# Block sums on VectorE, an earlier second product's transfer, and plain weight loads in a four-stage fp32 network step

## The chip, the core and the metric

The kernel runs on one core of a Trainium2 chip. TensorE multiplies, VectorE and ScalarE work element by element, POOL (GpSimd) does so too and issues the transfers of its queue, SP only issues transfers. The metric is the time of one execution on the device in microseconds.

## The reference, cut to what matters

640 tokens (512 latent, 128 context) of width 1024 pass through two layers. Each layer is a SwiGLU feed-forward, a token mixer (attention in layer 0, a long convolution in layer 1), and a second feed-forward, each with a modulation ahead of it and a layer norm behind. All is float32.

```python
def swiglu(h, w1, w2):
    g, u = jnp.split(h @ w1, 2, axis=-1)
    return (jax.nn.silu(g) * u) @ w2          # 1024 -> 2 x 2816 -> 1024

h = modulate(x, mod[:, 0], mod[:, 1])
f = swiglu(h, P['ffn_w1'][i, 0], P['ffn_w2'][i, 0])
x = layer_norm(DEEPNORM_ALPHA * x + 0.5 * mod[:, 2][:, None] * f, ...)
```

There are four feed-forwards: (layer 0, 0), (0, 1), (1, 0) and (1, 1). The modulation vectors `mod` come from one product of the condition with a 1024 x 9216 matrix per layer.

## The kernel before, in words

**Precision.** A float32 product is made of three passes over operands cut in a high and a low half (`hi`, `lo`): hi x hi, hi x lo, lo x hi. For a weight unit the high half `wh` comes by a transfer on POOL's queue that rounds it (`w_dma`, L115); the low half `wl` is made by `w_split`: ScalarE writes minus the high half into a new buffer (L127), and a second transfer of the same weights, accumulating, adds the full value (L128). Activations and block sums are cut by `split`: ScalarE copies the high half (L95), VectorE subtracts it (L96).

**Buffers and order.** All weight tiles, and the tiles `sw` below, share 8 buffers of 8 KB per partition (tag `w`). Every engine runs its instructions strictly in the order in which the program emits them; the order is written out by hand, and `w_get` splits units ahead as long as fewer than three are alive. `wlim` bounds how far weights may be loaded.

**Feed-forwards of layer 0** (`ffn`). The hidden layer has 22 columns of 128 in four parts of 6, 6, 6 and 4. For each column one unit of w1 (1 MB) is multiplied in two halves of 320 tokens (`ffn1`, L563, 96 matmuls); after a part's columns come four units of w2 (768 KB, `w2a`, L524, 72 matmuls each). Beside the work runs a background job, `bg_step`: a 512 KB piece of the modulation matrix (`ar`, double-buffered, issued by POOL at L243) is reduced on VectorE in two passes (L257). A column carries two steps; a w2 unit of the first two parts of feed-forward (0, 1) carries four. That feed-forward is the "prior" one: the block stages follow it.

**Feed-forwards of layer 1** (`ffn_s`), called block stages here. Columns 0 to 2 and 21 are computed as above. The 18 others go by a Strassen form in seven half-size products (`s_unit`): 84 matmuls at L669 of 128x128 weights with 320 tokens, each product of 12. Its weights are the four blocks a11, a12 (gate), a21, a22 (up) of a column, three of them as such (a11, a12, a22) and four sums s1 = a21 + a22, s2 = s1 - a11, s3 = a11 - a21, s4 = a12 - s2. `s_weights(c, nxt)` prepares them in four steps p0 to p3 during the column before; `hooks[i]` runs a step after product i. The raw blocks come by `s_load` on SP's queue into tiles `sr`. A block as such goes the way of a weight unit (copy, minus copy, accumulating transfer, L619 to L621); a sum is made on POOL or VectorE (L628, L635, L636, L645) and cut by `split`. The first product's result is copied by ScalarE (L685); further adds are VectorE's (L678, L699, L709).

Three columns make a part. Then `second` multiplies by two units `w2c` (768 KB; two of 1 MB, `w2b`, at the end): 16 groups of 9 matmuls at L524, eight for each unit; step `between[n]` runs after group n. The first of the two `w2c` units is loaded at `hooks[4]` of the part's second column and the other at `hooks[0]` of the third; the first is split at `hooks[2]` of the third, the other when `second` begins. In the last part, the next unit is column 21's w1 (1 MB).

Of the kernel before, what the change touches and what calls it, by code (L numbers as in the profile page):

```python
# [9 lines left out]
F32 = mybir.dt.float32  # L10
# [14 lines left out]

PARTS7 = [(0, 3), (3, 6), (6, 9), (9, 12), (12, 15), (15, 18), (18, 22)]
# [18 lines left out]
class Kernel:  # L45
# [63 lines left out]
    def w_dma(self, upto):  # L109
        nc = self.nc  # L110
        while self.wd < min(upto, self.wlim):
            i = self.wd
            src, shape = self.units[i]
            r = self.wp.tile(shape, F32R, tag="w", name="wh")
            nc.gpsimd.dma_start(out=r, in_=src)  # L115
            self.raw[i] = r
            self.wd += 1

    def w_split(self):
# [4 lines left out]
        shape = self.units[i][1]  # L124
        hi = self.raw.pop(i)
        lo = self.wp.tile(shape, F32R, tag="w", name="wl")
        self.nc.scalar.activation(out=lo, in_=hi.bitcast(F32), func=AF.Copy, scale=-1.0)  # L127
        self.nc.gpsimd.dma_start(out=lo, in_=self.units[i][0], accum_op=ALU.add)  # L128
# [5 lines left out]
    def w_first(self):  # L134

        i = self.wd
        src, shape = self.units[i]
# [459 lines left out]
    def s_load(self, blocks):  # L597

        for c, g, r in blocks:
            x = self.sp.tile([P, 4, P], F32, tag="sr", name="sr", bufs=5)  # L600
            self.nc.sync.dma_start(out=x, in_=self.I["w1s"][self.sf, c, g, r])
            self.sraw[c, g, r] = x

    def s_weights(self, c, nxt):

        nc = self.nc
        A = self.sraw
        st = {}
        self.sops[c] = ops = {}

        def slot(names):
            t = self.wp.tile([P, 4, 4, P], F32R, tag="w", name="sw")
            for i, n in enumerate(names):
                ops[n] = (t[:, i], t[:, 2 + i])

        def block(n, g, r):
            h, l = ops[n]
            x = A.pop((c, g, r)) if n == "a22" else A[c, g, r]
            nc.scalar.activation(out=h, in_=x, func=AF.Copy)  # L619
            nc.scalar.activation(out=l, in_=x, func=AF.Copy, scale=-1.0)  # L620
            nc.gpsimd.dma_start(out=l, in_=self.I["w1s"][self.sf, c, g, r], accum_op=ALU.add)  # L621

        def p0():
            st["s"] = self.sp.tile([P, 2, 4, P], F32, tag="s13", name="s13")
            st["d"] = self.sp.tile([P, 4, P], F32, tag="s24", name="s24")
            slot(("a11", "a12"))
            block("a11", 0, 0)
            nc.gpsimd.tensor_tensor(out=st["s"][:, 1], in0=A[c, 1, 0], in1=A[c, 1, 1], op=ALU.add)  # L628
            block("a12", 0, 1)
            if nxt is not None:  # L630
                self.s_load([(nxt, 0, 0)])
# [1408 lines left out]
```

## Time and profile before

| | us |
|---|---|
| median of 3 runs (2885.68 to 2892.03) | 2889.41 |
| profiled execution | 2896.11 |
| its span | 2893.1 |
| TensorE busy | 2648.9 (92%) |
| VectorE busy | 1709.7 (59%) |
| ScalarE busy | 1043.8 (36%) |
| POOL busy | 887.7 (31%) |

The span is that from the first to the last instruction of the profiled execution; 3.0 us lie around it. TensorE's granted clock is 0.960 of full speed over the span. POOL's queue moves 359.11 MB, SP's and the other hardware queue 89.72 MB. A busy share is an average over stages; what an idle stretch costs is read where it lies.

### The profile page before, as it was taken

The page shows a single profiled execution, that of the slowest core. Times are in us where ns is not written, and L with a number is a line of the kernel's source. Part 1 is how long each engine was busy: PE and PEld are TensorE (multiplying, and loading weights), DVE is VectorE, ACT ScalarE, POOL GpSimd, SP SyncE. Part 2 cuts the span into 40 slices and gives each one's busy share as a digit, 9 for nine tenths or more (in the row PEclk, how much of TensorE's full clock was granted, in tenths as well). Part 3 has the DMA queues.
Part 4 walks back from the last instruction along what each step waited for, and adds up shares of the span by engine and source line. Part 5 has one row for each costly group of instructions (what it writes and reads, how often), then busy time and mean ns, then how long its engine had stood idle before and what let it go on. Part 6 is the DMA issues. An engine that isn't in the chain of part 4 may idle for free.

```text
span 2893.1 us, 43816 instructions
## 1 busy us (share of the span) xinstructions
PE 2648.9 (92%) x16970; PEld 2505.6 (87%) x16970; DVE 1709.7 (59%) x3564; ACT 1043.8 (36%) x1916; POOL 887.7 (31%) x1126
## 2 busy tenths in 40 slices
PE   8799999999899988979998999989999898888887
PEld 3689999999548988979998999989999898888887
DVE  6846554449763556655377556546349758655554
ACT  4752212236773312111244333335323344333332
POOL 3521221143114211212153222224129643222223
PEclk9899999999999999989998999999999999999998
DMA  7877987862105678688645655564753544665552
GB/s 241 215 204 215 254 244 217 230 158 61 46 1 153 166 214 237 194 242 233 181 98 117 136 123 137 121 150 117 181 157 111 171 114 86 135 141 127 127 123 69
DMA packets 118214, 451.66 MB, mean 156 GB/s; under 512 B 13951, under 2 KB 19663, under 8 KB 93176
## 3 DMA queue, kind: packets, MB, share of 16 engines
q0 software_dynamic: 76800, 359.11, 49.7%
q1 hardware_dynamic: 40840, 89.72, 9.4%
q8 instruction: 134, 2.20, 0.3%
q14 instruction: 72, 0.59, 0.1%
q10 hardware_dynamic: 368, 0.04, 0.0%
HBM read 426.78 MB, written 16.01 MB: 153 GB/s over the span
## 4 chain that ended last, share of the span: by engine, by line
PE 51%; issue 21%; DVE 11%; DMA 7%; POOL 6%; ACT 4%; SPq 0%; POOLq 0%; DVEq 0%; ACTq 0%
PE f L524 18%; PE g L563 8%; PE u L563 8%; PE u L524 5%; PE sm L669 4%; DMA wl<-w2c 2%; PE o L1061 2%; PE pt L1050 1%; DMA wl<-w 1%; DVE s L635 1%; POOL ar L243 1%; POOL wh L115 1%; PE adar L211 1%; POOL s L628 1%; POOL sw L621 1%
## 5 line engine op out<-in xcount | busy, mean ns | idle before, releaser
L505 DVE SCALAR_TENSOR_TENSOR x<-f,gate,x 128x192 f32<-128x192 f32 (+2 forms) x576 | 227.1, 435 | 277.0 <-PE f L524 276.4
L524 PE MATMUL f<-sa,wh 128*128 128x320 f32 (+2 forms) x1344 | 321.9, 328 | 15.9 <-DVE sa L96 9.7
L127 ACT ACTIVATE wl<-wh 128x2048 fp32r<-128x2048 f32 (+1 forms) x131 | 229.0, 1748 | 275.0 <-PE f L524 185.1
L563 PE MATMUL g<-hh,wl 128*128 128x320 f32 (+1 forms) x832 | 262.2, 315 | 58.1 <-DMA wl<-w 58.1
L524 PE MATMUL f<-sa,wl 128*128 128x320 f32 (+2 forms) x672 | 222.6, 331 | 69.8 <-DMA wl<-w2c 63.0
L669 PE MATMUL sm<-st,sw 128*128 128x320 f32 x1728 | 261.4, 309 | 5.6 <-DMA sw<-w1s 5.6
L524 PEld LDWEIGHTS f<-sa,wh 128*128 128x128 f32 x1344 | 247.0, 206 | 18.0 <-DVE sa L96 10.2
L563 PE MATMUL g<-hh,wh 128*128 128x320 f32 (+1 forms) x832 | 262.1, 315 | 0.0
L669 PEld LDWEIGHTS sm<-st,sw 128*128 128x128 f32 x1728 | 254.9, 188 | 7.7 <-DMA sw<-w1s 7.7
L563 PE MATMUL u<-hh,wh 128*128 128x320 f32 (+1 forms) x832 | 260.6, 313 | 0.0
L563 PE MATMUL u<-hl,wh 128*128 128x320 f32 (+1 forms) x832 | 260.6, 313 | 0.0
L563 PE MATMUL u<-hh,wl 128*128 128x320 f32 (+1 forms) x832 | 260.5, 313 | 0.0
L563 PE MATMUL g<-hl,wh 128*128 128x320 f32 (+1 forms) x832 | 260.2, 313 | 0.0
L243 POOL DMA_DIRECT2D ar<-ada_w x128 | 67.9, 531 | 575.4 <-DVE mods L257 555.7
L621 POOL DMA_DIRECT2D sw<-w1s x108 | 106.2, 983 | 427.7 <-ACT sw L620 252.7
L524 PE MATMUL f<-ah,wl 128*128 128x320 f32 (+2 forms) x736 | 228.1, 310 | 2.7 <-DMA wl<-w2a 2.7
L524 PE MATMUL f<-al,wh 128*128 128x320 f32 (+2 forms) x736 | 228.6, 311 | 2.1 <-DVE al L96 1.6
L524 PE MATMUL f<-ah,wh 128*128 128x320 f32 (+2 forms) x736 | 229.0, 311 | 0.0
L257 DVE CUSTOM_DVE_ANT_0 prod<-ar,cond,ab 128x1024 f32<-128x1024 f32 x128 | 163.9, 1280 | 104.2 <-DMA ar<-ada_w 101.1
L563 PEld LDWEIGHTS g<-hh,wl 128*128 128x128 f32 x832 | 159.4, 192 | 60.5 <-DMA wl<-w 60.5
L572 DVE TENSOR_TENSOR ac<-sg,u 128x320 f32<-128x320 f32 (+1 forms) x104 | 50.5, 486 | 260.4 <-ACT sg L570 260.4
L524 PEld LDWEIGHTS f<-sa,wl 128*128 128x128 f32 x672 | 138.3, 206 | 73.2 <-DMA wl<-w2c 65.8
(359 smaller groups left out, 7052.3 us busy)
## 6 DMA issues: line engine op xcount, KB each, us to landing
ar<-ada_w POOLq DMA_DIRECT2D x128, 512.0 KB, 5.9
wh<-w POOLq DMA_DIRECT2D x50, 1024.0 KB, 11.5
wl<-w POOLq DMA_DIRECT2D x50, 1024.0 KB, 10.3
sr<-w1s SPq DMA_DIRECT2D x144, 256.0 KB
sw<-w1s POOLq DMA_DIRECT2D x108, 256.0 KB, 4.6
wh<-w2a POOLq DMA_DIRECT2D x24, 768.0 KB, 11.1
wl<-w2a POOLq DMA_DIRECT2D x24, 768.0 KB, 9.3
wh<-w2c POOLq DMA_DIRECT2D x24, 768.0 KB, 8.8
```

The costliest lines, as they stand in the source:

```text
L115: nc.gpsimd.dma_start(out=r, in_=src)
L127: self.nc.scalar.activation(out=lo, in_=hi.bitcast(F32), func=AF.Copy, scale=-1.0)
L211: nc.tensor.matmul(acc[ch][:2, :], self.sc[:, k, :], w[:, r, ch * 512:(ch + 1) * 512], start=(k == 0), stop=(k == 7))
L243: self.nc.gpsimd.dma_start(out=self.ada_raw[n], in_=self.I["ada_w"][l, m, j])
L257: nc.vector.tensor_tensor_reduce(out=out, in0=w, in1=self.cond[:, tk], scale=1.0, scalar=self.ab[:, l, m, j:j + 1], op0=ALU.mult, op1=ALU. ...
L505: nc.vector.scalar_tensor_tensor(out=self.x[:, j, s0:s1], in0=ps[:, s0 - a:s1 - a], scalar=gate[:, tk, j:j + 1], in1=self.x[:, j, s0:s1], ...
L524: nc.tensor.matmul(ps[:, 0:z - a], s[:, kw, c0:c0 + P], m[:, a:z], start=(first and i == 0 and q == 0), stop=(last and i == n - 1 and q == 2))
L563: nc.tensor.matmul(o[:, 0:z - a], s[:, k, c0:c0 + P], m[:, a:z], start=(k == 0 and q == 0), stop=(k == 7 and q == 2))
L572: nc.vector.tensor_tensor(out=ac, in0=sg, in1=uu[:, 0:z - a], op=ALU.mult)
L621: nc.gpsimd.dma_start(out=l, in_=self.I["w1s"][self.sf, c, g, r], accum_op=ALU.add)
L669: nc.tensor.matmul(ps[:, 0:320], s[:, k], x, start=(k == 0 and q == 0), stop=(k == 3 and q == 2))
L1061: nc.tensor.matmul(ob[R[r], :], v[:, vs[c], g * 64:(g + 1) * 64], pts.pop((b, g, c)), start=(c == 0), stop=(c == len(vs) - 1))
```

## The change

It has three pieces. First, in `s_weights`, all four block sums are made on VectorE; raw blocks come in pairs of 512 KB (two of 256 KB each in one transfer, three buffers instead of five), and the copies, minus copies, splits and accumulating transfers of two blocks are one instruction where their tiles lie side by side. Second, in the block stages the two units of the second product are loaded at `hooks[2]` and `hooks[3]` of a part's second column and split at `hooks[0]` and `hooks[3]` of its third; the last part's third unit is loaded at `hooks[2]` of the third column; the steps within `second` move from groups 1, 4, 7, 10 to 0, 3, 8, 11. Third, the w1 units of columns 3, 5, ..., 17 of feed-forward (0, 1) are loaded plainly on SP's queue into a third tile, and both halves come from it by `split` in two pieces of 128x1024. The host lays out `w1s` to fit (the up blocks in the order a22, a21).

```diff
+PLAIN = range(3, 18, 2)
@@ w_dma
-            src, shape = self.units[i]
-            r = self.wp.tile(shape, F32R, tag="w", name="wh")
-            nc.gpsimd.dma_start(out=r, in_=src)
+            src, shape, plain = self.units[i]
+            if plain:
+                r = self.wp.tile(shape, F32, tag="w", name="wr")
+                nc.sync.dma_start(out=r, in_=src)
+            else:
+                r = self.wp.tile(shape, F32R, tag="w", name="wh")
+                nc.gpsimd.dma_start(out=r, in_=src)
@@ w_split
+        if plain:
+            raw, hi = hi, self.wp.tile(shape, F32R, tag="w", name="wh")
+            for k in (slice(0, KD // 2), slice(KD // 2, KD)):
+                self.split(hi[:, k], lo[:, k], raw[:, k])
+        else:
+            self.nc.scalar.activation(out=lo, in_=hi.bitcast(F32), func=AF.Copy, scale=-1.0)
+            self.nc.gpsimd.dma_start(out=lo, in_=self.units[i][0], accum_op=ALU.add)
@@ s_load
-            x = self.sp.tile([P, 4, P], F32, tag="sr", name="sr", bufs=5)
-            self.nc.sync.dma_start(out=x, in_=self.I["w1s"][self.sf, c, g, r])
+        x = self.sp.tile([P, 2, 4, P], F32, tag="sr", name="sr", bufs=3)
+        self.nc.sync.dma_start(out=x, in_=self.I["w1s"][self.sf, c, h])
@@ s_weights
         def p0():
+            g, u = st["g"], st["u"] = A.pop((c, 0)), A.pop((c, 1))
+            s = st["s"] = self.sp.tile([P, 2, 4, P], F32, tag="ss", name="ss")
+            hi, lo = slot(("a11", "a12"))
+            nc.scalar.activation(out=hi, in_=g, func=AF.Copy)
+            nc.scalar.activation(out=lo, in_=g, func=AF.Copy, scale=-1.0)
+            nc.gpsimd.dma_start(out=lo, in_=src[0], accum_op=ALU.add)
+            tt(s[:, 1], g[:, 0], u[:, 1], ALU.subtract)
+            tt(u[:, 1], u[:, 1], u[:, 0], ALU.add)
+            tt(s[:, 0], u[:, 1], g[:, 0], ALU.subtract)
             if nxt is not None:
+                self.s_load(nxt, 0)
         def p1():
+            self.split(*slot(("s2", "s3")), st["s"])
+        def p2():
+            g, u, s = st["g"], st["u"], st["s"]
+            tt(s[:, 0], g[:, 1], s[:, 0], ALU.subtract)
+            hi, lo = slot(("a22", "s1"))
+            nc.scalar.activation(out=hi, in_=u, func=AF.Copy)
+            nc.scalar.activation(out=lo[:, 0], in_=u[:, 0], func=AF.Copy, scale=-1.0)
+            nc.gpsimd.dma_start(out=lo[:, 0], in_=src[1][:, 0], accum_op=ALU.add)
+            tt(lo[:, 1], u[:, 1], hi[:, 1].bitcast(F32), ALU.subtract)
             if nxt is not None:
+                self.s_load(nxt, 1)
         def p3():
-            self.split(*ops["s4"], st["d"])
+            self.split(*slot(("s4",)), st["s"][:, 0:1])
@@ ffn_s
                 if i == 1:
-                    def cast(m=u + 1):
-                    hooks[4] = cast
+                    hooks[2] = lambda m=u + 1: cast(m)
+                    hooks[3] = lambda m=u + 2, w=w: (w[2](), cast(m))
                 if i == 2:
-                    def cast(m=u + 2):
-                    hooks[0] = cast
-                    hooks[2] = self.w_split
+                    hooks[0] = self.w_split
+                    hooks[3] = self.w_split
+                    if fin:
+                        hooks[2] = lambda m=u + 3: cast(m)
-                second(u, acts, gt, {1: w[0], 4: w[1], 7: w[2], 10: w[3]})
+                second(u, acts, gt, {0: w[0], 3: w[1], 8: w[2], 11: w[3]})
@@ add_ffn_units
-                units.append((I["w1"][l, f, c], [P, KD, 256]))
+                units.append((I["w1"][l, f, c], [P, KD, 256], f == 1 and c in PLAIN))
...
```

In the diff `tt` is a VectorE `tensor_tensor`, and `slot` hands out the high and the low side of a tile `sw` of 8 KB per partition.

## Rows read from the trace of the kernel before

**Rows 1.** Busy time of each engine in stretches of the span, one line for each: feed-forward (0, 0), feed-forward (0, 1), block stage 1, block stage 2. Columns: stretch, its length, busy time and instructions of TensorE's matmuls, weight loads, VectorE, ScalarE and POOL, granted clock, DMA share, GB/s.

```profile
165.00:620.00 455.00, 453.96 (x3087) 453.04 (x3087) 227.16 (x430) 113.11 (x158) 96.48 (x149) 1.00 0.78 219
...
945.00:1430.00 485.00, 441.89 (x2914) 439.19 (x2913) 269.44 (x507) 106.02 (x143) 94.07 (x149) 0.95 0.76 214
1430.00:1970.00 540.00, 484.69 (x3161) 478.14 (x3160) 323.06 (x654) 202.43 (x379) 176.94 (x194) 0.95 0.52 120
...
2360.00:2893.00 533.00, 462.04 (x3003) 455.13 (x3001) 318.79 (x644) 192.31 (x366) 158.97 (x173) 0.93 0.50 113
```

**Rows 2.** What TensorE waited for: first a line of feed-forward (0, 1), then three of block stage 1, then two of block stage 2. Columns: waiting tile and line, who released it, total us, times, longest us.

```profile
PE g L563 <- DMA wl<-w: 40.3, 7, 10.0
...
PE f L524 <- DMA wl<-w2c: 32.1, 5, 7.9
PE g L563 <- DMA wl<-w: 9.2, 1, 9.2
...
PE f L524 <- DMA wl<-w2b: 3.4, 1, 3.4
...
PE f L524 <- DMA wl<-w2c: 30.9, 6, 6.7
PE g L563 <- DMA wl<-w: 8.6, 1, 8.6
```

**Rows 3.** Stretches from one resumption of TensorE to the next in the second product, eight parts of the two block stages; the first, and the sum of all eight. Columns as in rows 1.

```profile
1589.61:1656.09 66.48, 59.92 (x396) 59.40 (x397) 39.36 (x75) 25.07 (x48) 18.27 (x20) 0.96 0.57 131
...
sum 538.58, PE 485.15 PEld 480.71 DVE 314.80 ACT 202.60 POOL 147.72; mean PE 60.64 PEld 60.09 DVE 39.35 ACT 25.32 POOL 18.46
```

**Rows 4.** Timeline of TensorE in one part of block stage 1: the four middle products (48 matmuls) of the second and the third column, and the matmul that waited. Columns: start, length, engine, line, operation, tiles, count, and in brackets the idle time before it and its releaser.

```profile
1559.64 7.20 PE L669 MATMUL sm<-st,sw 128*128 128x320 f32 x48
...
1571.96 7.20 PE L669 MATMUL sm<-st,sw 128*128 128x320 f32 x48
...
1589.61 0.63 PE L524 MATMUL f<-sa,wl 128*128 128x320 f32 x1 [7.89 <-DMA wl<-w2c]
```

**Rows 5.** Timeline of ScalarE in the same part: the copies of the three columns' first products, and the minus copy of the second product's first unit.

```profile
1545.82 0.44 ACT L685 ACTIVATE s<-sm 128x320 f32<-128x320 f32 x1 [2.27 <-PE sm L669]
...
1561.95 0.42 ACT L685 ACTIVATE s<-sm 128x320 f32<-128x320 f32 x1
...
1578.06 0.42 ACT L685 ACTIVATE s<-sm 128x320 f32<-128x320 f32 x1
...
1581.14 1.48 ACT L127 ACTIVATE wl<-wh 128x1536 fp32r<-128x1536 f32 x1 [1.56 <-DMA wh<-w2c]
```

**Rows 6.** Timelines of VectorE (the first line) and POOL (the others) in the same part.

```profile
1549.82 2.69 DVE L635 TENSOR_TENSOR s<-s,sr 128x512 f32<-128x512 f32 x1 [1.74 <-POOL s L628]
...
1548.15 1.63 POOL L628 TENSOR_TENSOR s<-sr 128x512 f32<-128x512 f32 x1
...
1550.01 1.95 POOL L636 TENSOR_TENSOR s<-sr 128x512 f32<-128x512 f32 x1
...
1571.79 1.41 POOL L115 DMA_DIRECT2D wh<-w2c  x2
1582.92 0.88 POOL L128 DMA_DIRECT2D wl<-w2c  x1 [9.72 <-ACT wl L127]
```

**Rows 7.** Durations over the whole span of the operations on the tiles `sw` and `sr`: count, then least/median/greatest ns, first and last start, shapes.

```profile
L96 DVE TENSOR_TENSOR sw<-s,sw x144: 681/685/695, 1540.0 to 2802.7; 128x512 fp32r<-128x512 f32 x144
...
L635 DVE TENSOR_TENSOR s<-s,sr x36: 681/2686/2714, 1537.3 to 2793.1; 128x512 f32<-128x512 f32 x36
...
L96 DVE TENSOR_TENSOR sa<-s,sa x36: 491/492/495, 1558.2 to 2809.3; 128x320 fp32r<-128x320 f32 x36
```

**Rows 8.** The page's list of transfers: tiles, queue, count, size of one, median us from issue to landing.

```profile
ar<-ada_w POOLq DMA_DIRECT2D x128, 512.0 KB, 5.9
wh<-w POOLq DMA_DIRECT2D x50, 1024.0 KB, 11.5
...
wh<-w2c POOLq DMA_DIRECT2D x24, 768.0 KB, 8.8
```

**Rows 9.** Feed-forward (0, 1), from the second product of its first part into the next part's columns: timelines of POOL (three lines), VectorE (one) and TensorE (three; in three successive columns the first matmul of the low half, which waited for it).

```profile
1052.67 0.91 POOL L128 DMA_DIRECT2D wl<-w2a  x1
...
1072.07 0.91 POOL L128 DMA_DIRECT2D wl<-w  x1
...
1113.49 0.91 POOL L128 DMA_DIRECT2D wl<-w  x1
...
1066.09 1.28 DVE L257 CUSTOM_DVE_ANT_0 prod<-ar,cond,ab 128x1024 f32<-128x1024 f32 x1 [6.30 <-DMA ar<-ada_w]
...
1082.53 0.64 PE L563 MATMUL g<-hh,wl 128*128 128x320 f32 x1 [9.41 <-DMA wl<-w]
...
1103.82 0.64 PE L563 MATMUL g<-hh,wl 128*128 128x320 f32 x1 [4.77 <-DMA wl<-w]
...
1124.32 0.41 PE L563 MATMUL g<-hh,wl 128*128 128x320 f32 x1 [4.33 <-DMA wl<-w]
```

**Rows 10.** TensorE in short stretches behind waits: stretch, length, busy time and matmuls, granted clock, DMA share, GB/s.

```profile
1927.10:1930.10 3.00, 3.00 (x11) 0.50 0.94 191
1931.00:1934.00 3.00, 3.00 (x23) 1.00 1.02 360
1082.60:1085.60 3.00, 3.00 (x11) 0.50 1.00 401
```

More of the change, by code (lines that the diff above doesn't have):

```diff
@@ L123, in w_split @@
         self.w_dma(i + 1)
-        shape = self.units[i][1]
+        shape, plain = self.units[i][1:]
         hi = self.raw.pop(i)
         lo = self.wp.tile(shape, F32R, tag="w", name="wl")
-        self.nc.scalar.activation(out=lo, in_=hi.bitcast(F32), func=AF.Copy, scale=-1.0)
-        self.nc.gpsimd.dma_start(out=lo, in_=self.units[i][0], accum_op=ALU.add)
+        if plain:
[5 more added lines that the diff above has]
+            self.nc.gpsimd.dma_start(out=lo, in_=self.units[i][0], accum_op=ALU.add)
         self.wt[i] = (hi, lo)
@@ L136, in w_first @@
         i = self.wd
-        src, shape = self.units[i]
+        src, shape = self.units[i][:2]
         self.raw[i] = self.wp.tile(shape, F32, tag="w", name="wr")
@@ L607, in s_weights @@
         A = self.sraw
+        src = self.I["w1s"][self.sf, c]
+        self.sops[c] = ops = {}
         st = {}
-        self.sops[c] = ops = {}
         def slot(names):
             t = self.wp.tile([P, 4, 4, P], F32R, tag="w", name="sw")
[L613 to L621, printed above, removed]
@@ L623, in p0 @@
-        def p0():
[L624 to L629, printed above, removed]
+            n = len(names)
+            for i, x in enumerate(names):
+                ops[x] = (t[:, i], t[:, n + i])
+            return t[:, 0:n], t[:, n:2 * n]
@@ L630, in p0 @@
             if nxt is not None:
-                self.s_load([(nxt, 0, 0)])
+                self.s_load(nxt, 0)
         def p1():
-            slot(("s2", "s3"))
-            nc.vector.tensor_tensor(out=st["d"], in0=st["s"][:, 1], in1=A[c, 0, 0], op=ALU.subtract)
-            nc.gpsimd.tensor_tensor(out=st["s"][:, 0], in0=A.pop((c, 0, 0)), in1=A.pop((c, 1, 0)), op=ALU.subtract)
-            self.split(*ops["s2"], st["d"])
-            self.split(*ops["s3"], st["s"][:, 0])
-            if nxt is not None:
-                self.s_load([(nxt, 1, 0)])
@@ L642, in p2 @@
-        def p2():
-            slot(("a22", "s1"))
-            block("a22", 1, 1)
-            nc.vector.tensor_tensor(out=st["d"], in0=A.pop((c, 0, 1)), in1=st["d"], op=ALU.subtract)
-            self.split(*ops["s1"], st["s"][:, 1])
-            if nxt is not None:
-                self.s_load([(nxt, 1, 1), (nxt, 0, 1)])
+            self.split(*slot(("s2", "s3")), st["s"])
[7 more added lines that the diff above has]
+            tt(lo[:, 1], u[:, 1], hi[:, 1].bitcast(F32), ALU.subtract)
+            if nxt is not None:
+                self.s_load(nxt, 1)
@@ L650, in p3 @@
         def p3():
-            slot(("s4",))
-            self.split(*ops["s4"], st["d"])
+            self.split(*slot(("s4",)), st["s"][:, 0:1])
         return [p0, p1, p2, p3]
@@ L761, in ffn_s, with cast @@
                 hooks = {}
+                def cast(m):
+                    self.wlim = m
+                    self.w_dma(m)
                 if i < 2:
@@ L1840, in run @@
                 self.add_ffn_units(units, l, 1)
-            self.w_init(units)
+            self.w_init([(x + (False,))[:3] for x in units])
             self.consts()
```

17 lines of the change are left out of this document (8 added, 9 removed).

## The prediction

> **What bounds the kernel now.** I read the windows by stage first, then who TensorE waited for in each stage, then the windows from one stall to the next, then the timelines of every engine round one stall. In the first feed-forward TensorE is busy for 454.0 of 455 us at a granted clock of 1.00, so an undisturbed stage has nothing to give; the three stages that the change touches lose 43, 55 and 71 us of TensorE time [rows 1]. What TensorE waits for there is almost one thing: the low half `wl` of a weight, made by a copy on ScalarE and then an accumulating transfer from POOL's queue [rows 2].
>
> *The block stages.* From stall to stall a part takes 538.58 / 8 = 67.3 us [rows 3]. A column's 84 matmuls take 12.32 us (1559.64 to 1571.96), 0.1467 each [rows 4], so the 396 matmuls of a part (3 x 84 and 144) need 58.1: each part loses 9.2 us, 6.3 of it the wait (32.1 + 30.9 over ten parts, [rows 2]) and the rest the clock after it and small waits. After a wait of 9.2 us there are 11 matmuls in 3 us at a granted clock of 0.50 (1.2 GHz), then 23 in 3 us at 1.00 (2.4 GHz) [rows 10]; about 3.1 us at half rate, 1.5 us lost.
>
> The wait is the end of a lag. ScalarE copies the first product of a column; the copies come at 1545.82, 1561.95 and 1578.06, 16.1 us apart [rows 5], while TensorE goes at 12.3. The third column's middle products start at 1571.96 [rows 4], its first product ended two products earlier, near 1570.2, and is copied 8 us late. The lag grows by 4 us a column, and the chain shows why: POOL's sum (1.63), VectorE's difference held to 2.69 beside POOL's next operation (1.95) [rows 6], and ScalarE and VectorE, strictly in order, behind it. In that late queue stands the copy for `wl`: it starts at 1581.14, POOL issues the transfer at 1582.92 [rows 5, 6], TensorE goes on at 1589.61 after 7.89 us [rows 4]; issue to use is 6.7.
>
> *The prior feed-forward.* While its second product runs, each weight unit carries four background steps (`ar`, two VectorE passes each) on double buffers. VectorE waits for `ar`, POOL for VectorE, and the weight transfers stand behind both in POOL's queue: POOL reaches the weights of successive units at 1052.67, 1072.07 and, two units on, 1113.49, some 20 us a unit, against 72 matmuls x 0.1467 = 10.6 us of TensorE. Waits of 9.41 and 4.77 us follow, and the third unit starts at 1124.32 [rows 9].
>
> **The change, part by part.**
>
> *1. Block sums and pairs.* Out: two POOL operations (1.63 and 1.95 us), one accumulating issue of three, the 2.69 us form. In on VectorE for one column: three sums, one more difference, one 128x512 low half on its own for s1 and one for s4, six of 0.685 [rows 7], and one low half of 128x1024 (not in the trace; below two of 0.685 = 1.37, above one; I take 1.2, being one instruction's start less): 5.3 us. The two ends of a sum are 0.68 and 2.69 [rows 7]; the long one stands beside POOL's 1.95, and 0.68 + 1.95 is nearly all of it. With no POOL arithmetic left in a column I take 0.68; with 2.69 four sums would cost 8 us more, 18.7 in 12.3, and the lag would be worse than now (rival A). The Trainium skill (SBUF — State Buffer, Who interferes with whom) says that a VectorE instruction with two SBUF inputs and a POOL instruction that reads SBUF exclude each other; the trace agrees so far (2.69 beside 1.95). By that rule the long form can't come back, since POOL only issues transfers in a column, and the sum is the 0.68 one.
>
> Eleven operations of 128x320 at about 0.49, as the column has already, add 5.4: 10.7 us in 12.3. Hand-offs with ScalarE (about 0.55 four times) bring it to about 12.9, so the lag grows by 0.6 a column, not 4. What delays the next column's first copy is the end of this one: the seventh product is there at 12.32 + 0.4, an add, a SiLU and a multiplication (0.5 each, with hand-offs) lead to ScalarE's split of `sa` at 14.4, with the second column's 0.6 at 15.0, which is 2.7 into the third. The first copy follows at about 3.1 after the third column's start; its input is ready at 2.2, and now it comes at 9.7 (1578.06 less 1568.4).
>
> Issues move too: the second half of a column's raw block load now waits for the last reads of the pair before. It leaves about 9 us into the column; with 5.9 us for a 512 KB transfer [rows 8] it lands at 14.9, 2.6 into the next, where VectorE wants it at 3.1. Hidden by half a microsecond; SP has nothing else behind it but the next such load.
>
> *2. The second product's transfers, a column earlier.* `wh` 1 goes behind the first pair's accumulate, about 5.8 us into column 2 (its slot has long been free), and lands 8.8 us later [rows 8] at 14.6, that is 2.3 into column 3; the 512 KB ahead of it may make that 4.2. The `wl` copy (1.48, [rows 5]) then ends between 4.6 and 5.7, POOL issues 0.3 later, and 6.7 later, at 11.6 to 12.7, `wl` is there. TensorE wants it at 12.3 + 0.3. So the wait is 0 to 0.1, and up to 2 where the transfer shares the engines with `wh` 2. I keep 1.5 us a part: each gives 7.7, ten parts **77**. `wl` 2 is copied in column 3 instead of at the start of the second product; it wasn't waited for and costs nothing, since ScalarE has some 7 free microseconds in that column. If that cover went, the split of `sa` behind it would be late by 1.5.
>
> The last part's `wl` are 1 MB. `wh` lands later (11.5 instead of 8.8, [rows 8]), so of the waits of 9.2 and 8.6 [rows 2] about 2 each and a low clock stay: 8.9 and 1.5 now, 3.5 then, 2 x 6.9 = **14**. The waits of 3.4 behind them (w2b; the other stage's is the same to 0.1) each with 1.5 of clock go but for 1: **8**.
>
> *3. Eight plain loads.* Each takes 1 MB of accumulate away and moves the other 1 MB to SP; in come two VectorE operations of 1.2 (2.4 us) and the same ScalarE time. In the stalled stretch the plain units are the second (column 7, 13) and fourth. So at POOL one unit's wait sequence carries 768 KB in place of 1.77 MB, and one carries nothing. The `ar` behind 1.77 MB keeps VectorE idle for 6.30 us [rows 9]; in proportion to the bytes the first gives 3.6, the other 6.3 less 2.4 of VectorE's new work, 3.9. SP's megabytes take back between 0 and all of the 7.5; I take 2.5, for a load of 1 MB by 11.5 us [rows 8] lies beside only a part of these waits. That leaves 5 us by which the third unit starts earlier, and 1.5 of clock for a stall fewer: twice 6.5 = **13**. The second unit's own stall goes (nothing for it is in POOL's queue), but the third waits longer for it: that is where most of the 40.3 us [rows 2] stays. Cost if SP's loads aren't hidden: the gain is gone.
>
> Sum: 77 + 14 + 8 + 13 = 112. The profiled execution took 2896.11 us (span 2893.1 and 3.0 round it), which gives 2784. The median of the runs is 6.7 below that execution, so by it **2777**.
>
> Bounds: everything in items 1 and 2 gone is 92 + 21 + 10 = 123, and 25 for item 3, 148 in all: 2742. Under 0.2% (5.8 us) a measurement can't be told from no change.
>
> **Rivals.**
>
> *A. The lag stays.* VectorE at 10.7 of 12.3 us, in order, with every hand-off to ScalarE in line, may lag as far as now. Then only the copy's place (two small operations earlier) counts, 1 to 3 us a part. For it: 87% load without any queue slack. Against it: the 4 us of growth are all at POOL's sum and the 2.69. Ten parts x 2, plus 10 elsewhere: 30 us, **2860**; with half the lag, 2825.
>
> *B. Plain loads buy nothing.* `ar` transfers share the DMA engines with SP's megabyte and land as late as now; VectorE's 2.4 us sit in the same chain. For it: DMA shares near 1.0 stand in this stage too [rows 10]; against it: POOL's queue is shorter in any case. Items 1 and 2 stay: 2889 - 99 = **2790**, and 2806 if the 2.4 and a few us of sharing cost both stretches. The Trainium skill (DMA: Bandwidth & Descriptors, Queues, rings and completion order) has the rule that speaks for it: a DMA engine takes turns between the queues that have work, so a load on another queue isn't free for those on POOL's. By that rule item 3 is nearer to 0 than to 13. No row here has an SP megabyte beside `ar`.
>
> *C. Slower: the raw block load.* VectorE's sums stand first in line in column 2; if the second half of the load isn't there, everything behind them stops. Up to 6.4 us (5.9 and the 0.5 to spare) nothing happens, and each us more is one of lag. The `wl` copy would start at 3.4 into column 3 and starts near 9.9 at best now, so from 13 us on it is as late as now; at 18 us each of ten parts waits 5 longer: 50 more, less 13, **2926**. Against it: no 512 KB median here is over 5.9, and one load in each part is so tight.
>
> *D. More.* All the waits go, the prior stage's too: **2742**.
>
> **How the numbers follow.** Forecast 0.62 (own range 2758 to 2798: 0 to 3.5 us left in each of ten parts), A 0.15, B 0.11, C 0.04, D 0.08. Predicted is the forecast's 2777. The range 2745 to 2840 holds the forecast, B, most of D and the lower third of A. Faster by over 0.2%: all but C and a remainder, 0.95; within 0.2%: 0.02; slower: 0.03.
>
> **What would show it.** Right: no POOL arithmetic in a column; VectorE's sums at 0.68; ScalarE's first copies 12 to 13 us apart; the `wl` copy within 6 us of the third column's start; parts near 59.6 us; the w2c waits under 15 us in all; in the prior stage two stalls instead of three in each stretch, the second column without one. Wrong: copies still 16 us apart (A), VectorE waiting for `sr` (C), POOL at 20 us a unit in the whole stalled stretch (B). The forecast is wrong most easily through the lag: each us of it beyond 4 comes back in ten parts.

## The result and the profile after

The changed kernel takes **2762.65 us** (median of four runs, 2758.91 to 2765.61) against 2890.68 for the kernel before (four runs, 2885.68 to 2892.03): a ratio of **0.9559**, 95% interval [0.9543, 0.9576], 128.0 us. The forecast was 2777 and the range 2745 to 2840. The profiled execution of the changed kernel took 2762.68 us with a span of 2760.7.

Where the 132.4 us between the two spans lie is read from three events that both traces have: TensorE's first matmul of a second product in each block stage (it waits for `sa`), and the layer norm behind the first stage.

| stretch | before | after | gain |
|---|---|---|---|
| start to the first second product of block stage 1 | 1521.71 | 1512.44 | 9.3 |
| from there to the layer norm (`rs`) | 448.85 | 389.26 | 59.6 |
| from there to the same event of block stage 2 | 440.54 | 438.83 | 1.7 |
| from there to the end of the span | 482.0 | 420.2 | 61.8 |

The windows of these stretches, first of the kernel before, then of the changed one (columns as in [rows 1]):

```profile
1521.80:1970.50 448.70, 399.15 (x2577) 394.25 (x2577) 260.85 (x518) 164.76 (x304) 128.33 (x135) 0.94 0.55 126
2411.20:2893.00 481.80, 416.05 (x2691) 410.40 (x2691) 278.35 (x568) 171.62 (x320) 134.34 (x142) 0.93 0.52 118
```

```profile
1512.50:1901.60 389.10, 381.87 (x2577) 379.65 (x2577) 259.00 (x536) 158.07 (x232) 65.36 (x81) 0.99 0.60 145
2340.60:2760.60 420.00, 401.16 (x2691) 398.15 (x2691) 276.57 (x586) 164.88 (x248) 71.53 (x88) 0.97 0.55 135
```

The matmuls are the same in number; they take 32.2 us less because the granted clock is 0.99 and 0.97 in place of 0.94 and 0.93. VectorE's busy time has hardly changed, although it has taken over all sums; POOL's has halved. TensorE's waits in the same two windows, answering [rows 2]:

```profile
PE g L573 <- DMA wl<-w: 1.7, 1, 1.7
PE f L534 <- DMA wl<-w2c: 1.7, 2, 1.3
...
PE f L534 <- DMA wl<-w2b: 0.4, 1, 0.4
...
PE f L534 <- DMA wl<-w2c: 1.4, 1, 1.4
PE g L573 <- DMA wl<-w: 0.6, 1, 0.6
```

In these windows the kernel before waited 62.6 us for w2c, 17.8 for column 21's weights, 6.8 for w2b and 6.4 for `sw`; the changed one waits 3.1, 2.3, 0.4 and 0. That is 87.8 us of waits, and with the 32.2 of clock 120 of the 121.4 us gained in the two stages.

One part of block stage 1, ScalarE (copies of the first products and, at L137, the minus copy for the second product), answering [rows 5]:

```profile
1653.36 0.44 ACT L692 ACTIVATE s<-sm 128x320 f32<-128x320 f32 x1 [9.11 <-PE sm L676]
1665.85 0.42 ACT L692 ACTIVATE s<-sm 128x320 f32<-128x320 f32 x1
1679.02 0.42 ACT L692 ACTIVATE s<-sm 128x320 f32<-128x320 f32 x1
1679.34 1.48 ACT L137 ACTIVATE wl<-wh 128x1536 fp32r<-128x1536 f32 x1
```

The copies are 12.5 and 13.2 us apart (16.1 before). The third column starts at 1676.04 (its middle products at 1679.56, less 3.52), so its copy comes 3.0 us into the column and the minus copy 3.3 (4.5 in the part before, 5.7 in the first). VectorE in block stage 1, grouped by shape (busy, mean ns, then idle time ahead), and the one place where it waited long for a raw block:

```profile
L629 DVE TENSOR_TENSOR ss<-sr 128x512 f32<-128x512 f32 x36 | 24.8, 688 | 1.8 <-DMA sr<-w1s 1.1
L97 DVE TENSOR_TENSOR sw<-ss,sw 128x1024 fp32r<-128x1024 f32 x18 | 22.0, 1223 | 17.9 <-ACT sw L96 17.8
...
1608.83 0.69 DVE L629 TENSOR_TENSOR ss<-sr 128x512 f32<-128x512 f32 x1 [1.11 <-DMA sr<-w1s]
```

The sums are at 0.69 and the long low half at 1.22. Three windows from one second product into the next:

```profile
1571.71:1630.46 58.75, 58.35 (x396) 58.09 (x397) 39.00 (x78) 23.82 (x35) 8.02 (x10) 1.00 0.64 150
1630.46:1689.15 58.69, 58.69 (x400) 58.69 (x401) 39.28 (x78) 24.16 (x36) 7.98 (x10) 1.00 0.62 150
2401.42:2459.90 58.48, 58.48 (x399) 58.48 (x399) 38.87 (x77) 23.70 (x34) 8.04 (x10) 1.00 0.63 151
```

The first holds the 396 matmuls of a part and a wait of 0.40; the other two hold 400 and 399, which makes 58.1 and 58.0 us for 396, with TensorE never idle.

In the prior feed-forward TensorE still waits. First its weight stalls in the changed kernel, answering [rows 9] (the second column's is gone; the 3.68 for the unit of w2 ahead of them was 1.15 in the kernel before), then VectorE's waits for `ar`, of the changed kernel and of the kernel before:

```profile
1064.66 0.64 PE L534 MATMUL f<-ah,wl 128*128 128x320 f32 x1 [3.68 <-DMA wl<-w2a]
1082.99 0.64 PE L573 MATMUL g<-hh,wl 128*128 128x320 f32 x1 [5.04 <-DMA wl<-w]
1119.38 0.63 PE L573 MATMUL g<-hh,wl 128*128 128x320 f32 x1 [6.09 <-DMA wl<-w]
```

```profile
1049.24 1.29 DVE L267 CUSTOM_DVE_ANT_0 prod<-ar,cond,ab 128x1024 f32<-128x1024 f32 x1 [8.13 <-DMA ar<-ada_w]
1065.91 1.29 DVE L267 CUSTOM_DVE_ANT_0 prod<-ar,cond,ab 128x1024 f32<-128x1024 f32 x1 [3.49 <-DMA ar<-ada_w]
1088.59 1.29 DVE L267 CUSTOM_DVE_ANT_0 prod<-ar,cond,ab 128x1024 f32<-128x1024 f32 x1 [9.75 <-DMA ar<-ada_w]
```

```profile
1046.69 1.29 DVE L257 CUSTOM_DVE_ANT_0 prod<-ar,cond,ab 128x1024 f32<-128x1024 f32 x1 [5.37 <-DMA ar<-ada_w]
1086.29 1.28 DVE L257 CUSTOM_DVE_ANT_0 prod<-ar,cond,ab 128x1024 f32<-128x1024 f32 x1 [6.95 <-DMA ar<-ada_w]
```

SP's plain loads in this first stretch of the changed kernel go out at 1039.60 and 1077.58; behind each of them one `ar` is waited for 2.8 us longer than before (8.13 against 5.37, 9.75 against 6.95). In the second stretch it is 0.9 and 1.6 longer (6.76 against 5.89, 9.14 against 7.52). Where the accumulating transfer is missing the wait is 2.81 shorter (3.49 against 6.30, [rows 9]).

### The profile page after: what moved, and what is told of

The parts are those of the page before. It is cut to its first block, busy times and chain, and to the rows that moved or that the text cites. A ratio compares the mean times of both kernels' runs of the same rounds, so it can differ in the third digit from the quotient of the medians.

```text
span 2760.7 us, 43283 instructions
## 1 busy us (share of the span) xinstructions
PE 2611.2 (95%) x16970; PEld 2472.4 (90%) x16970; DVE 1722.9 (62%) x3616; ACT 1031.3 (37%) x1780; POOL 752.7 (27%) x1002
## 5 line engine op out<-in xcount | busy, mean ns | idle before, releaser
L534 PE MATMUL f<-sa,wh 128*128 128x320 f32 (+2 forms) x1344 | 304.0, 313 | 15.8 <-DVE sa L97 10.6
L137 ACT ACTIVATE wl<-wh 128x2048 fp32r<-128x2048 f32 (+1 forms) x123 | 214.0, 1740 | 271.2 <-PE f L534 161.3
L534 PEld LDWEIGHTS f<-sa,wh 128*128 128x128 f32 x1344 | 230.1, 192 | 17.6 <-DVE sa L97 11.1
L534 PE MATMUL f<-sa,wl 128*128 128x320 f32 (+2 forms) x672 | 210.4, 313 | 3.5 <-DMA wl<-w2c 3.1
L676 PE MATMUL sm<-hh,sw 128*128 128x320 f32 x864 | 197.9, 309 | 0.0
L580 ACT ACTIVATE sg<-g 128x320 f32<-128x320 f32 (+1 forms) x104 | 45.1, 434 | 341.2 <-PE g L573 341.1
## 6 DMA issues: line engine op xcount, KB each, us to landing
wh<-w2a POOLq DMA_DIRECT2D x24, 768.0 KB, 10.8
```

Of the source, the lines that this page charges most:

```text
L534: nc.tensor.matmul(ps[:, 0:z - a], s[:, kw, c0:c0 + P], m[:, a:z], start=(first and i == 0 and q == 0), stop=(last and i == n - 1 and q == 2))
L580: nc.scalar.activation(out=sg, in_=g[:, 0:z - a], func=AF.Silu)
L676: nc.tensor.matmul(ps[:, 0:320], s[:, k], x, start=(k == 0 and q == 0), stop=(k == 3 and q == 2))
```

## The experiments

Gains are against the kernel before, run beside each kernel on the same chip (medians 2889.95, 2893.97 and 2892.32 in the three sets). By that measure the whole change is worth 128.0.

| kernel | median us | gain | ratio and interval |
|---|---|---|---|
| sums and pairs alone | 2806.67 | 83.3 | 0.9712 [0.9696, 0.9728] |
| moved transfers alone | 2858.99 | 31.0 | 0.9884 [0.9860, 0.9909] |
| plain loads alone | 2880.99 | 9.0 | 0.9972 [0.9958, 0.9986] |
| sums on VectorE, no pairs | 2796.44 | 93.5 | 0.9679 [0.9661, 0.9698] |
| change + 2.75 us on VectorE a column | 2848.61 | 45.4 | 0.9839 [0.9821, 0.9856] |
| change + unread POOL operations | 2785.39 | 108.6 | 0.9623 [0.9608, 0.9638] |
| change, first sum on POOL | 2874.47 | 17.9 | 0.9940 [0.9918, 0.9962] |
| change, steps spread | 2738.07 | 155.9 | 0.9460 [0.9441, 0.9478] |
| change, `ar` from SP | 2732.50 | 161.5 | 0.9440 [0.9422, 0.9458] |
| change, both | **2725.09** | **167.2** | 0.9421 [0.9402, 0.9440] |
| change, `ar` from SP, no plain loads | 2740.23 | 152.1 | 0.9472 [0.9454, 0.9491] |
| change, both, no plain loads | 2739.30 | 153.0 | 0.9465 [0.9443, 0.9487] |

### The three pieces apart

**Sums and pairs alone.** The changed kernel's `s_load` and `s_weights` with the old hooks:

```diff
-PLAIN = range(3, 18, 2)
+PLAIN = ()
-                    hooks[2] = lambda m=u + 1: cast(m)
-                    hooks[3] = lambda m=u + 2, w=w: (w[2](), cast(m))
+                    hooks[4] = cast
...
-                    hooks[0] = self.w_split
-                    hooks[3] = self.w_split
+                    hooks[0] = cast
+                    hooks[2] = self.w_split
-                second(u, acts, gt, {0: w[0], 3: w[1], 8: w[2], 11: w[3]})
+                second(u, acts, gt, {1: w[0], 4: w[1], 7: w[2], 10: w[3]})
```

> The block sums on VectorE and the pairs alone; the transfers of the second product stay where they were, no plain loads. My theory (the waits for w2c are the end of a lag that POOL's sum and the VectorE difference held beside POOL's next operation build up): first-product copies 12.5 to 13.5 us apart, the third column's copy about 3 us after its column starts, the `wl` copy about 6 us after it in place of 12.7, so the low half is there near 14.5 to 15 where TensorE wants it at 12.6: about 2 us of wait a part in place of 6.3, parts near 61.5, and 55 to 85 of the 126 us of the whole change. Rival (the place of the transfers is what counts): at most 30 us.

Measured: 83.3, at the upper end. ScalarE in one part:

```profile
1608.12 0.44 ACT L692 ACTIVATE s<-sm 128x320 f32<-128x320 f32 x1 [10.30 <-PE sm L676]
1620.61 0.42 ACT L692 ACTIVATE s<-sm 128x320 f32<-128x320 f32 x1
1633.76 0.42 ACT L692 ACTIVATE s<-sm 128x320 f32<-128x320 f32 x1
1636.34 1.49 ACT L137 ACTIVATE wl<-wh 128x1536 fp32r<-128x1536 f32 x1 [0.76 <-DMA wh<-w2c]
```

The copies are already 12.5 and 13.2 apart. The minus copy comes 2.6 us after the third one, where it waits 0.76 for its `wh`, and the waits for w2c are 13.9 us in ten parts, in place of 63.

**Moved transfers alone.** The reverse edit: the new hooks and steps in the kernel before.

> The earlier loads and splits of the second product's units alone; the sums stay on POOL and VectorE as before. My theory: copies still 16 us apart, the third column's copy still 9.7 us after its start, so the `wl` copy is only some 2.5 us earlier than before (it stands behind that copy): 20 to 40 us in all. Rival (the place of the transfers is what counts): 90 us or more.

Measured: 31.0, as my theory had it.

```profile
1612.46 0.44 ACT L685 ACTIVATE s<-sm 128x320 f32<-128x320 f32 x1 [9.10 <-PE sm L669]
1628.54 0.42 ACT L685 ACTIVATE s<-sm 128x320 f32<-128x320 f32 x1
1644.62 0.42 ACT L685 ACTIVATE s<-sm 128x320 f32<-128x320 f32 x1
1644.94 1.48 ACT L127 ACTIVATE wl<-wh 128x1536 fp32r<-128x1536 f32 x1
```

The copies are still 16.1 apart, and the minus copy goes out right behind the late third one. The waits for w2c halve to 31.4 us in ten parts, but 13 us come back as waits for `sw` (19.4 against 6.4). The likely reason, which no run tests, is that the steps are put elsewhere in a chain that is as late as before.

**Plain loads alone.** `PLAIN`, `w_dma`, `w_split` and the `units` of the changed kernel in the kernel before.

> The eight plain loads of feed-forward (0, 1) alone. The forecast's step: 13 us faster. From the trace of the changed kernel: 9 us, all of it ahead of the block stages. Rival (the transfers for `ar` share the engines with SP's megabyte and eat all of it): within 3 us of no change.

Measured: 9.0, and the event that ends the prior stage comes at 1512.71, 9.0 before that of the kernel before. The three pieces alone sum to 123.3 of 128.0. That nearly fits, but not because they are independent: of the 63.0 us of waits for w2c the first removes 49.1 alone and the second 31.6 alone, together more than there is, and the 13 us of `sw` waits that the second brings when it is alone are gone in the change.

**Sums without pairs.** Single blocks, five raw buffers and three accumulating transfers as before; two words change:

```diff
-            nc.gpsimd.tensor_tensor(out=st["s"][:, 1], in0=A[c, 1, 0], in1=A[c, 1, 1], op=ALU.add)
+            nc.vector.tensor_tensor(out=st["s"][:, 1], in0=A[c, 1, 0], in1=A[c, 1, 1], op=ALU.add)
-            nc.gpsimd.tensor_tensor(out=st["s"][:, 0], in0=A.pop((c, 0, 0)), in1=A.pop((c, 1, 0)), op=ALU.subtract)
+            nc.vector.tensor_tensor(out=st["s"][:, 0], in0=A.pop((c, 0, 0)), in1=A.pop((c, 1, 0)), op=ALU.subtract)
```

> Only the two POOL sums of a column go to VectorE; blocks stay single, with three copies, three minus copies and three accumulating transfers, and all transfers where they were. My theory: VectorE's 2.69 us form is 0.68, VectorE carries about 11 us of a column's 12.3, the copies are 12.5 to 13.5 us apart as in the kernel with pairs, and the gain is that of sums and pairs less at most 15 us. Rival (the number of instructions and issues, halved by the pairs, is what keeps the engines behind): copies 14.5 us apart or more and under half of the gain of sums and pairs.

Measured: 93.5, not less than with pairs.

```profile
1657.63 0.44 ACT L685 ACTIVATE s<-sm 128x320 f32<-128x320 f32 x1 [9.84 <-PE sm L669]
1670.12 0.42 ACT L685 ACTIVATE s<-sm 128x320 f32<-128x320 f32 x1
1682.44 0.42 ACT L685 ACTIVATE s<-sm 128x320 f32<-128x320 f32 x1
...
L635 DVE TENSOR_TENSOR s<-s,sr 128x512 f32<-128x512 f32 x18 | 12.3, 683 | 0.0
```

The copies are 12.5 and 12.3 apart, TensorE's own pace, and L635, 2.69 in [rows 7], is 0.683. So moving two sums does the work of piece 1, and the pairs add nothing: the kernel without them is 10.2 us faster, with no overlap between the runs of the two (2794.11 to 2801.56, 2804.88 to 2807.90). Of the 10 us between the two medians the block stages account for 3 (93.3 gained there without pairs, 90.4 with them, by the same events as above); most of the rest is in the prior stage, which is the same code in both, and ends 5.9 us apart in the two profiles; why it does was not found.

### What made the lag

**VectorE's dose.**

```diff
-            tt(s[:, 1], g[:, 0], u[:, 1], ALU.subtract)
+            for _ in range(5):
+                tt(s[:, 1], g[:, 0], u[:, 1], ALU.subtract)
```

> The changed kernel, with the first block sum of every Strassen column made five times: four idempotent VectorE operations of 0.69 us more in each column, 2.75 us, nothing else. My theory (VectorE with its hand-offs is the chain that sets a column's pace, 12.5 to 13.2 us now, so it has no slack for 2.75): copies 15 to 16 us apart, the third column's copy at about 8 us after its start instead of 3.0; by the prediction's last sentence each us beyond 4 comes back in ten parts: 40 us and up to 55 with the clock and the three other waits, 2803 to 2820. Rival (a column has slack; what counted was POOL and the late place of the transfers): under 10 us slower, copies 13.5 apart at most.

Measured: 82.7 of the 128.0 lost, half as much again as the upper end of what was expected.

```profile
1666.67 0.44 ACT L693 ACTIVATE s<-sm 128x320 f32<-128x320 f32 x1 [9.10 <-PE sm L677]
1681.05 0.42 ACT L693 ACTIVATE s<-sm 128x320 f32<-128x320 f32 x1
1697.11 0.42 ACT L693 ACTIVATE s<-sm 128x320 f32<-128x320 f32 x1
...
1707.18 0.63 PE L534 MATMUL f<-sa,wl 128*128 128x320 f32 x1 [5.05 <-DMA wl<-w2c]
...
1771.02 0.63 PE L534 MATMUL f<-sa,wl 128*128 128x320 f32 x1 [3.68 <-DMA wl<-w2c]
```

The copies are 14.4 and 16.1 apart, 1.9 and 2.9 more than in the change for 2.75 of added work: the first of the two columns had some 0.9 us of slack, the other none. The mechanism per part holds: 37.9 us of waits for w2c in ten parts (3.1 in the change), and 62.4 to 64.9 us a part in stage 1 and 64.6 to 65.1 in stage 2 where the change has 58.6, so some 5.3 and 6.2 in each; the third column's copy is 7.8 us in (its middle products start at 1692.87). What the expectation left out is the rest: waits for column 21's weights of 5.8 and 6.0 (2.3 in all in the change), new waits for `sw` at the start of each stage, 4.8 and 3.7, and the clock behind all of them, 0.95 and 0.92 in the two stages, at which the same matmuls last 32.9 us longer.

**POOL beside VectorE.** Two POOL operations a column whose result nobody reads:

```diff
+            nc.gpsimd.tensor_tensor(out=self.dummy, in0=g[:, 0], in1=g[:, 1], op=ALU.add)
+            nc.gpsimd.tensor_tensor(out=self.dummy, in0=g[:, 0], in1=g[:, 1], op=ALU.subtract)
             tt(s[:, 1], g[:, 0], u[:, 1], ALU.subtract)
```

> The changed kernel, with two POOL operations of 128x512 put back into every Strassen column whose results nobody reads (they read the raw block and write a scratch tile): what stood beside VectorE before, without the dependence on it. Theory 1 (POOL and VectorE exclude each other, and that made the lag): VectorE operations beside them last 2 to 2.7 us, copies 14.5 to 16.5 us apart, 20 to 50 us slower than the changed kernel. Theory 2 (only the wait for POOL's result made the lag): copies 12.5 to 13.5 apart, within 10 us of the changed kernel. The forecast leaned on both at once and did not divide the 4 us between them.

Measured: 19.4 of the 128.0 lost, between the two theories. POOL and VectorE in one column:

```profile
1660.61 1.63 POOL L639 TENSOR_TENSOR dummy<-sr 128x512 f32<-128x512 f32 x1
1662.33 2.17 POOL L640 TENSOR_TENSOR dummy<-sr 128x512 f32<-128x512 f32 x1
...
1661.24 2.10 DVE L97 TENSOR_TENSOR sw<-ss,sw 128x1024 fp32r<-128x1024 f32 x1 [1.49 <-ACT sw L96]
```

The low half that takes 1.22 alone takes 2.10 here, beside the end of POOL's first operation and the start of its second, which itself is held to 2.17 (the same subtraction takes 1.62 in the next kernel, where VectorE stands still). Over block stage 1 VectorE's operations on raw blocks and sums last 15.7 us longer, 0.87 a column, and the copies are 13.4 apart; the w2c waits stay at 6.2 in ten parts. The loss is mostly at the edges of the stages: 4.5 and 4.0 for `sw` early in each, 3.7 more than in the change for column 21's weights, 3.1 more for w2c, and 7.6 by which the same matmuls last longer at the lower clock. The Trainium skill (SBUF — State Buffer, Who interferes with whom) has the two engines hold a shared pair of ports in turn, as a lock; the trace agrees, 2.10 against 1.22. It is a real cost, but in this place, where no operation waits for POOL's result, it does not make the 4 us of a column.

**One sum on POOL.** The first block sum again, now with VectorE dependent on it. VectorE's next sum, in place in `u[:, 1]`, overwrites a block that POOL's sum reads, so it can't start before that has ended:

```diff
-            tt(s[:, 1], g[:, 0], u[:, 1], ALU.subtract)
+            nc.gpsimd.tensor_tensor(out=s[:, 1], in0=g[:, 0], in1=u[:, 1], op=ALU.subtract)
```

> The changed kernel with the first block sum of a column made on POOL again (the other three stay on VectorE): a dependence on POOL, whose sum stands behind an accumulating issue that waits for ScalarE's copies. POOL operations beside VectorE without a dependence cost 22 us and 0.9 us of VectorE a column. Theory (the dependence was most of the 4 us a column): copies 14.5 to 16 us apart, the third column's copy 6 to 9 us after its start, 40 to 85 us slower than the changed kernel. Rival (a single dependence is absorbed; it took the two POOL sums and the exclusion together): copies under 14 us apart, at most 25 us slower.

Measured: 110.1 of the 128.0 lost, more than expected. POOL, then VectorE in one column:

```profile
1691.08 0.86 POOL L637 DMA_DIRECT2D sw<-w1s  x1 [8.61 <-ACT sw L636]
1691.65 1.62 POOL L638 TENSOR_TENSOR ss<-sr 128x512 f32<-128x512 f32 x1
...
1693.30 0.69 DVE L629 TENSOR_TENSOR sr<-sr 128x512 f32<-128x512 f32 x1 [4.21 <-POOL ss L638]
```

POOL's sum takes 1.62 us and saves VectorE 0.69. But it stands in POOL's queue behind the issue of an accumulating transfer, which waits for ScalarE's two copies; VectorE stands still for 4.21 us (62.0 us in 16 places of block stage 1), and the copies are 16.75 apart (1671.72, 1688.47, 1705.21), 0.6 more than in the kernel before. One dependence gives back nearly the whole change. It is not quite the one of the kernel before: the two copies that POOL's queue waits for are those of a pair, 1.05 us each in place of 0.62.

### The prior feed-forward

**Steps spread.** Three background steps in a w1 column and two in a w2 unit, in place of two and four:

```diff
             if bg:
                 self.bg_step()
+                if last and bg > 1:
+                    self.bg_step()
...
-                self.run_steps(..., c > 0)
+                self.run_steps(..., (c > 0) * (1 + f))
...
                         self.bg_step()
-                        if pi < 2 and f:
-                            self.bg_step()
```

> The changed kernel, with the background steps of feed-forward (0, 1) spread: three in a w1 column and two in a w2 unit, instead of two and four (78 places for 72 steps). The stalls left there in the changed kernel are six of 2.95 to 6.55 us and two of 2.6 and 3.7 at the w2 units, some 33 us, and about 8 us of low clock. My theory (four pieces in one w2 unit are more than the transfers can bring in 10.6 us: 3.5 MB, 330 GB/s, against 360 to 400 at best; spread it is 236 to 248): stalls under 12 us, 20 to 30 us faster than the changed kernel. Rival (POOL's queue waits for VectorE's buffers wherever the steps stand): under 8 us.

Measured: 27.9 us faster than the change. TensorE's weight waits in that feed-forward (936 to 1400 us) are 5.5 for w2 and 3.2 for w1 in place of 6.2 and 26.7, and the stage ends 26.9 us earlier (1485.56). The number is the expected one, but its reason, too many bytes, does not hold: the next kernel leaves the bytes where they were.

**`ar` from SP's queue.**

```diff
-            self.nc.gpsimd.dma_start(out=self.ada_raw[n], in_=self.I["ada_w"][l, m, j])
+            self.nc.sync.dma_start(out=self.ada_raw[n], in_=self.I["ada_w"][l, m, j])
```

> The changed kernel, with the transfers of the modulation matrix (`ar`) issued from SP's queue instead of POOL's, everywhere in the program; the four steps stay in a w2 unit. Theory 1 (the weights come late because POOL stands waiting for VectorE ahead of them): the stalls of feed-forward (0, 1) fall to under half, 15 to 25 us faster than the changed kernel. Theory 2 (the bytes are too many for that stretch, whoever issues them): within 6 us. This tells which of the two rows of the forecast's third step stood for: the queue or the engines.

Measured: 33.5 us faster than the change. TensorE's waits in the same window, first with `ar` from SP, then with both edits:

```profile
PE g L573 <- DVE x L515: 11.2, 4, 3.9
...
PE g L573 <- DMA wl<-w: 0.7, 1, 0.7
```

```profile
PE f L534 <- ACT ah L96: 7.4, 3, 5.6
PE g L575 <- DMA wl<-w: 0.6, 1, 0.6
```

The same bytes in the same w2 units arrive in time once POOL no longer stands waiting for VectorE's buffers ahead of a weight: 33 us of weight stalls become 0.7, and the stage ends 28.2 us earlier (1484.22). So the queue was the cause, not the bytes. What POOL waits for in the change, then ScalarE's minus copy of one weight and POOL's issue of the transfer that needs it, in the change and with `ar` from SP:

```profile
POOL ar L253 <- DVE mods L267: 301.5, 69, 12.9
...
1050.07 1.92 ACT L137 ACTIVATE wl<-wh 128x2048 fp32r<-128x2048 f32 x1 [9.07 <-PE f L534]
1071.88 0.91 POOL L138 DMA_DIRECT2D wl<-w  x1
```

```profile
1046.47 1.92 ACT L137 ACTIVATE wl<-wh 128x2048 fp32r<-128x2048 f32 x1 [9.07 <-PE f L534]
1048.69 0.88 POOL L138 DMA_DIRECT2D wl<-w  x1 [10.13 <-ACT wl L137]
```

The issue follows the end of the copy by 19.9 us in the change (up to 20.8) and by 0.3 with `ar` from SP. POOL's waits for VectorE's buffers weigh far more in it than its work of issuing, 0.53 us for an `ar`. That the spread helps nearly as much fits: fewer `ar` issues then stand ahead of a weight, and the issue is at most 10.9 us behind the copy.

**Both edits.**

> The changed kernel with both edits: `ar` issued from SP's queue, and three background steps in a column and two in a w2 unit of feed-forward (0, 1). With SP's queue alone TensorE no longer waits there for weights but 11.2 us for VectorE (the sum into `x` behind four background steps). Theory (the two waits are separate: the queue for the weights, the crowding of steps for VectorE): that wait goes too, 8 to 15 us faster than with SP's queue alone. Rival (the steps in a column hold up VectorE there instead): within 4 us of it.

Measured: 5.7 us faster than with SP's queue alone by gains, a little under what was expected; by the event that ends the stage 9.8 (1474.42 against 1484.22). The wait for VectorE's `x` is gone, and 7.4 us for ScalarE's split of `ah` have come. This is the fastest kernel of the study, 39.2 us faster than the change.

**Without plain loads.** `PLAIN = ()` in each of the last two kernels.

> The changed kernel with `ar` on SP's queue and no plain loads: all weights by a transfer and an accumulating one from POOL again. Theory (the plain loads helped only by taking bytes out of the queue in which POOL stood waiting for VectorE; with that wait gone they buy nothing): within 5 us of the kernel with `ar` on SP's queue and plain loads, and no weight stall over 3 us in feed-forward (0, 1). Rival (the accumulating transfers themselves are too many for the stretch): weight stalls of 15 us or more return.

> Both edits and no plain loads. Theory: within 4 us of the same kernel with plain loads, so the third piece of the change is replaced by the queue and the spread. Rival: more than 4 us slower, so the plain loads still carry something.

Measured: 9.4 and 14.2 us less gain than with plain loads. Both theories missed. No weight stall returned (0.8 in all with SP's queue alone), yet the plain loads are still worth something. In the first pair the profiles themselves differ by only 2.0 us at the end of the span, so its 9.4 is not located; what there is shows as TensorE's wait for VectorE's `x`, 15.6 in place of 11.2. In the second pair the prior stage ends 14.5 us later (1488.93), with 15.2 us for `ah` in place of 7.4. Why ScalarE is later there was not followed up and stays open.

## Why the prediction was right

**The lag** was the right cause. Sum (0.68 forecast, 0.69), long low half (1.2, 1.22), growth of a column (0.6; 0.2 and 0.9 in the part shown, up to 2.5 in the first two), the third copy (3.1 us in, 3.0) and the minus copy (3.1 to 4.2, 3.3) came as worked out; only in the first two parts of block stage 1 the minus copy was later, at 5.7 and 4.5. The sums-alone and moves-alone kernels divide the gain 83 to 31, as a lag would have it: the place of a transfer counts for less while the copy ahead of it is late.

**Where the 4 us of a column come from** was left undivided, and the runs divide it only in part. In the kernel before, VectorE's difference waits 1.74 us for POOL's sum in the second column of the part [rows 6] and 2.96 in the third:

```profile
1565.93 2.69 DVE L635 TENSOR_TENSOR s<-s,sr 128x512 f32<-128x512 f32 x1 [2.96 <-POOL s L628]
```

Both times it is then held 2.0 us longer than its 0.68, so in that arrangement the wait and the exclusion weigh about the same. Taken apart, a dependence is enough: one operation behind POOL's queue that VectorE must wait for costs it 4.21 us a column and gives back 110.1 us, while two POOL operations that nobody waits for cost VectorE 0.87 a column and 19.4 in all. But neither kernel has POOL's operations where they stood before, so the shares of the 4 us stay open.

**The term of w2c** was mis-sized: 77 forecast, with 1.5 us left in each part. From the first matmul of one second product to that of the next it is 59.7, 58.8, 58.1 and 58.1 us in block stage 1 and 59.7, 58.1, 58.1 and 58.1 in block stage 2, against the 58.1 that the matmuls need. What is left thus lies in the first part of each stage and the second of stage 1; the others lose nothing. The mean is 58.6, and ten parts at 67.3 less 58.6 make 87. The first low half still came 1.3 us late (1571.71, behind a minus copy at 1563.29) and in stage 2 1.4; the second by 0.4 in stage 1; the others not at all. Column 21's two waits went from 17.8 to 2.3 us where 4 were forecast to stay, and those for w2b to 0.4 where 1 each was. The waits for `sw`, 6.4 us, were in the forecast only as "small waits" of a part. The two stages gave 121.4 against 99, nearly the bound of 123.

**The plain loads** gave 9.3 where 13 was forecast. Third units start 4.9 us earlier in the first stretch (1119.38 against 1124.32; forecast 5) and a further 3.8 in the second, but no clock came back, since stalls of 3 to 6.6 us remain: over the prior stage the same matmuls are busy for 543.4 us (542.9 before). That 4.9 meets 5 is luck, for the terms were off both ways. The gain in bytes was 2.8 at the first unit (forecast 3.6). SP's megabytes took 2.8 each, 5.6 in the first stretch, where 2.5 was put. The unit with nothing in POOL's queue gave 5.7 where 3.9 was put: from the `ar` that is waited for ahead of it (1086.29 before, 1088.59 after) to POOL's issue for the third unit (1113.49 and 1110.10) it is 27.2 and 21.5 us. From that issue to its use it was 9.3 in place of 10.8, which the forecast did not have. Rival B's rule, that the engines take turns between queues, was thus half right. The Trainium skill (DMA: Bandwidth & Descriptors, Queues, rings and completion order) has the DMA engines take turns between the queues that have work, without a price. The traces agree, with 2.8 us for each `ar` beside 1 MB in the first stretch and 0.9 and 1.6 in the second.

**The other rivals.** A (the lag stays) fell with the copies 12.5 to 13.2 apart in the part shown, but the dose shows how near it was: VectorE did not have 2.75 us to spare. C (the raw block late) came once in the two block stages: in column 2 of the second part VectorE waited 1.11 us at 1608.83, the copies of that column were 14.4 apart in place of 13.2 (1607.10, 1621.48), and TensorE paid 0.40 at 1630.46. The half microsecond to spare was as small as put, and the price of a miss of this size is small too. D was nearly met in the block stages and not at all in the prior one.

## What to carry to other kernels

Before giving a small operation to an idle engine, look at what already stands in that engine's queue and what it waits for: a 1.6 us sum made VectorE stand still for 4.2 us in a column, and weights behind another transfer's buffer wait cost TensorE 33 us of stalls that another queue took away. Where a transfer comes late, first ask whether the copy ahead of it is late; moving the issues of a lagging chain gained 31.0 us alone, against 83.3 for removing the lag. A queue of issues with waits of two kinds in it is worth splitting before the bytes are cut.

## What the runs showed of the hardware that was not expected

- POOL's queue holds a transfer back when an issue ahead of it waits for a buffer: the issue for a weight came up to 20.8 us after the copy it needs, and 0.3 with `ar` on SP. Two issuing queues carried the same bytes without the stalls of one: with `ar` on SP the weight waits of the prior feed-forward fell from 32.9 to 0.7 us, at 213 GB/s against 203 over the same 464 us.
- VectorE and POOL delay each other in both directions: 2.10 in place of 1.22 us for VectorE's low half, and 2.17 for POOL's second operation where an unhindered one of the same shape took 1.62 to 1.63.
- One accumulating transfer and one copy for two blocks in place of two of each made nothing faster: sums with pairs measured 10.2 us slower than sums without, although ScalarE has 232 instructions in block stage 1 with the pairs and 304 before.
